# Layer B of a two-layer streaming encoder: the probabilities of head pairs 1 to 7 turned by DMA transposes in place of TensorE transposes

## The chip, the core and the metric

One Trainium2 chip, one core. The metric is the device time of one execution in microseconds (us). Three runs of the kernel before gave 2242.28, 2232.93 and 2240.86 us, a median of 2240.86 us. One further execution was recorded by the hardware profiler; all rows below are of that one.

## What is computed

Two attention layers over 2048 prompt tokens and 64 sample tokens, model width 1024. The change is in the second layer (layer B): 16 heads of 64 dimensions, a band of the token's own chunk and 8 earlier chunks of 64, a learned bias by clipped distance, and a gate. Cut to what matters:

```python
p = h @ w_in                                  # q, k, v, gate of layer B, 4 x 1024 columns
s = jnp.einsum('bqkgd,bskd->bkgqs', qg, k) * (dh ** -0.5) + bias
p = jax.nn.softmax(s, axis=-1)                # band of 9 chunks
o = jnp.einsum('bkgqs,bskd->bqkgd', p.astype(v.dtype), v)
y_p = x_p + (op * jax.nn.silu(gp)) @ w_out
```

All is float32 in the reference. The kernel gets there on TensorE by splitting a float32 operand into a high and a low part (here two float16 numbers) and multiplying both.

## The kernel before

**Stages.** Layer A's attention runs to about 0.69 ms of the profile, its output projection to about 0.9 ms, layer B's attention from there to about 2.08 ms, and the rest of layer B's output projection ends the program. Projections are not a stage of their own: `Filler` is a generator that hands out projection matmuls (`project`, L678 to L680, of 512 columns) a few at a time, and the pipelines of the two layers call `filler.to(mark)` between their own steps. The order of TensorE's instructions is therefore written out by hand (`manual_schedule` for PE); the other engines and the DMA queue of SyncE (SP), which issues every transfer, are ordered by a scheduler when the program is built.

**Layer B's pipeline.** `layer_b` makes one item for each head pair `hp` (0 to 7) and each unit of 256 tokens (8 units, each of two tiles of 128 tokens, and one sample item of 64 tokens). An item of a full unit has four steps, (tile i, head h) = (0,0), (1,0), (0,1), (1,1). A tile's band is up to five blocks of 128 keys: units 0 and 1 have 1, 2, 3 and 4 blocks for their tiles, all later ones 5. In one step:

- `scores` (L1408, L1409): four matmuls into a two-bank PSUM tile `sb`; VectorE adds the bias and takes the row minimum (L1412) into `p`, a 128x640 float32 tile of which there are three; ScalarE takes the exponential (L1416) and the row sum.
- one step later `values`: TensorE transposes each 128x128 float32 block of `p` into another `sb` tile (L840, the helper `transpose`); ScalarE writes the high part `ph` scaled by `PB` as float16 (L815), VectorE the low part `pl` (L816), both in `split_to`.
- after the second tile of a head, `products` (L1503): for each block of keys one matmul of `values` (held as `VH`) with `ph` and one with `pl`, 256 columns where both tiles see the block and 128 where one does. The first of them are put between the transposes of the next step's `values`; the rest, with two transposes of the gate `G` for the second head, follow them.
- at the end of the second head `finish_pairs` (L1243 to L1248) adds the halves, multiplies by the gate on GpSimd (POOL) and stores to `ogb`.

`queries` (L1347 to L1363) prepares the next item's q and k; `flush` issues copies of q (L1352) and stores held back. `Background` runs evacuation and normalisation work (`head_norm`: POOL at L755, L759 and L760, VectorE at L756 and L773) at fixed places; `anchor` names the ScalarE and VectorE instructions behind which such work is placed. Activations of layer B are loaded to `xx` from DRAM (L526, two transfers of 512 KB for each unit), through seven buffers. `VH` fills half of the `values` tile; the other half lies unused in layer B.

Of the kernel before, what the change touches and what calls it, by code (L numbers as in the profile page):

```python
# [11 lines left out]
F16 = mybir.dt.float16  # L12
I32 = mybir.dt.int32
AF = mybir.ActivationFunctionType
ALU = mybir.AluOpType
# [33 lines left out]
QY = 1  # L49
NS = 4  # L50
HB, WB_, PB, VB = 2.0 ** 10, 2.0 ** 14, 2.0 ** 14, 16.0
LAG = 3
HALF = 5 * 2 * P

@with_exitstack
def hybrid_encoder_kernel(
# [162 lines left out]
    def input_across(h):  # L219
        across(h, h + 1)  # L220
        e, r, o = row[:, 16:17], row[:, 17:18], row[:, 20:23]
        powers(row[:, h : h + 1], e, r)
        times(o[:, 0:1], r, WB_)
        times(o[:, 1:2], e, 1 / (HB * WB_))
        times(o[:, 2:3], e, 0.5 / (VB * PB))

    def input_scales(h):
        everywhere(h, row[:, 20:23])
# [581 lines left out]
    def split_to(dst_hi, dst_lo, src, scale=None):  # L810
# [7 lines left out]
            )  # L818
        return a, b

    def load_cache(ktsrc, vsrc, C, both):
# [12 lines left out]
        nt = C // P  # L834
        for c in range(nt):
            split_to(VS[:, c, :, 0:HD], VS[:, c, :, HD:P], rvv[:, c])
# [415 lines left out]
    def layer_b():  # L1252
# [4 lines left out]
        def add_unit(hp, unit):  # L1257
            u, T, tiles = unit
            it = Item()
            it.hp, it.unit, it.ready = hp, unit, False  # L1260
            its.append(it)
            last = u == NU
            cols = slice(2 * hp * HD, (2 * hp + 2) * HD)

            def prefetch():
                for j in range(NO):
                    assert finished["x1", j] == 2 or j * OT >= u * UT + T
                rows = None if hp else token_rows(unit)
                st.x[hp, u] = x = load_act(
                    x1, u * UT, T, False, T == TS, None, xs[1], hp > 0, F16, rows  # L1270
                )
                return x

            def weights(*m):
                if hp not in st.emit:
                    (st.w[hp],), _, st.emit[hp] = load_weights(1, (w_in_b[hp], 512), scale=gsb[:, hp])
                st.emit[hp](*m)

            def gen():
                xc = st.x.pop((hp, u))  # L1280
                it.prs, it.todo = [], []
                it.gate = t("pb", [P, 2, P], 5)
                if "VH" not in held:
                    held["VH"] = t("values", [P, NT, 2, P], 1, F16)
                for e, (tt, t0, n) in enumerate(tiles):
                    out = []
                    c = yield from project((tt, t0, n), xc, st.w[hp], 512, out)
                    if last:
                        pr, sums = evacuate_sample(hp, out[0], it.gate[:, e])
                        it.prs.append(pr)  # L1290
                        v, kn = pr[:n, 256:384], pr[n:, 0:128]
                        it.todo += [sums] + head_norm(P, pr[:, 0:128]) + gate(P, it.gate[:, e, 0:HD])
# [82 lines left out]
        def scores(it, i, h):  # L1375
# [35 lines left out]
            for r, b, c in soft:  # L1411
                mi = nc.vector.tensor_tensor_reduce(  # L1412
                    out=p[r, :nk], in0=S[r, o : o + nk], in1=b,
                    op0=ALU.add, op1=ALU.min, scale=1.0, scalar=3e38, accum_out=it.nm[r, c : c + 1],
                )
            ex = nc.scalar.activation(  # L1416
                p[:n, :nk], p[:n, :nk], AF.Exp,
                scale=-1.0, bias=it.nm[:n, c : c + 1], accum_out=it.sm[:n, c : c + 1],
            )
            bg.anchor(mi, ex)  # L1420
            if c == w - 1:
                nc.vector.reciprocal(it.sm[:n, :w], it.sm[:n, :w])
                it.G = G = t("G", [P, 256])
                if u == NU:
                    nc.gpsimd.tensor_tensor(
# [3 lines left out]
                for e in range(len(tiles)):  # L1429
                    nc.gpsimd.tensor_tensor(  # L1430
                        G[:n, e * P : (e + 1) * P].rearrange("p (h d) -> p h d", d=HD),
                        it.gate[:n, e].rearrange("p (h d) -> p h d", d=HD),
                        it.sm[:n, 2 * e : 2 * e + 2].unsqueeze(2).to_broadcast([n, 2, HD]),
                        op=ALU.mult,
                    )

        def values(it, i, h, short):
            u, T, tiles = it.unit
# [21 lines left out]
            ))  # L1460

        def then(it, i, h):
            if it.unit[0] == NU:
                return [([], lambda: sample_outputs(it)), ([], lambda: sample_turned(it))]
            if i == len(it.unit[2]) - 1:
                return [products(it, h)]
            return []

        def sample_outputs(it):
            O = psum("o", 512, 1)  # L1470
# [11 lines left out]
        def sample_turned(it):  # L1482
# [5 lines left out]
            store(og[1][:, it.hp, SEQ:TOK], o)  # L1488
            finished[1, NU] = finished.get((1, NU), 0) + 1

        def products(it, h):
            u, T, tiles = it.unit
            ta, tb = tiles[0][0], tiles[1][0]
# [16 lines left out]

            def rest():
                if h == 1:
                    n = tiles[0][2]
                    GT = psum("tp", 512, 1)
                    for e, (_, t0, _) in enumerate(tiles):
                        transpose(GT[:, t0 : t0 + n], it.G[:n, e * P : (e + 1) * P])
                    gt = gate_t(GT[:, :T].rearrange("p (j s) -> p j s", j=1), T, G_B(it.hp))
                for y, x in enumerate(full):
                    if y:
                        product(x, 0)  # L1520
                    product(x, 1, stop=y == last)
                if h == 1:
                    finish_pairs(
                        it.O[:, : 2 * T].rearrange("p (j e s) -> p j e s", j=1, e=2),
                        gt,
                        T,
                        og[1][:, it.hp : it.hp + 1, u * UT : u * UT + T],
                        True,
                    )
                    finished[1, u] = finished.get((1, u), 0) + 1  # L1530

            between = [begin]
            for x in short:
# [8 lines left out]
        def pipeline():  # L1542
# [7 lines left out]
            flush()  # L1550
            filler.to(its[1].mark)
            filler.attending = True
            prev, todo = None, []
            for x, it in enumerate(its):
                sample = it.unit[0] == NU
                heads = [(0, 0)] if sample else [(i, h) for h in range(2) for i in range(2)]
# [33 lines left out]
            values(*prev, [])  # L1590
            todo += then(*prev)
            while todo:
                filler.to(filler.done + 2.6)
                short, nxt = todo.pop(0)
                for fn in short:
                    fn()
                nxt()
            flush()

        return pipeline  # L1600
# [226 lines left out]
```

## Time and profile before

| | |
|---|---|
| median of three runs | 2240.86 us |
| profiled execution: its own time / span of its instructions | 2242.53 us / 2240.8 us |
| mean granted TensorE clock | 0.989 |
| share of the span busy: VectorE, ScalarE | 70%, 63% |
| share of time of the 16 DMA engines, SP's queue | 49.1% |
| bytes moved | 340.77 MB |

How to read it: TensorE's matmuls overlap one another, so the mean duration of a matmul in a group is longer than the time by which it moves the next one; the distance between the starts of neighbours in the timeline tells that. "Idle before" of a group is the idle time of its engine just before its instructions, with the instruction that ended it. SP's own row is a queue: a transfer that waits for a buffer holds up those behind it.

### The profile page before, as it was taken

The page shows a single profiled execution, that of the slowest core. Times are in us where ns is not written, and L with a number is a line of the kernel's source. Part 1 is how long each engine was busy: PE and PEld are TensorE (multiplying, and loading weights), DVE is VectorE, ACT ScalarE, POOL GpSimd, SP SyncE. Part 2 cuts the span into 40 slices and gives each one's busy share as a digit, 9 for nine tenths or more (in the row PEclk, how much of TensorE's full clock was granted, in tenths as well). Part 3 has the DMA queues.
Part 4 walks back from the last instruction along what each step waited for, and adds up shares of the span by engine and source line. Part 5 has one row for each costly group of instructions (what it writes and reads, how often), then busy time and mean ns, then how long its engine had stood idle before and what let it go on. Part 6 is the DMA issues. An engine that isn't in the chain of part 4 may idle for free.

```text
span 2240.8 us, 41683 instructions
## 1 busy us (share of the span) xinstructions
PE 2162.1 (96%) x13931; PEld 1580.2 (71%) x13931; DVE 1567.7 (70%) x4049; ACT 1419.6 (63%) x3610; POOL 858.4 (38%) x1397
## 2 busy tenths in 40 slices
PE   7999999999999999989999999999999999998999
PEld 6877888788889996556666666666566665566888
DVE  6768777667676456878776776867767777677542
ACT  6878778667785333666676666766666667566430
POOL 5545544334354456753333333332332323331000
PEclk9999999999999999999999999999999999999999
DMA  8856547756546666554243342533433424223664
GB/s 269 272 159 215 177 124 220 227 158 187 173 131 190 208 206 232 179 166 128 87 147 110 106 144 76 157 95 97 138 104 113 133 77 126 73 66 99 190 200 126
DMA packets 254072, 340.77 MB, mean 152 GB/s; under 512 B 45648, under 2 KB 191328, under 8 KB 253824
## 3 DMA queue, kind: packets, MB, share of 16 engines
q1 hardware_dynamic: 253856, 338.10, 49.1%
q8 instruction: 110, 1.80, 0.3%
q14 instruction: 106, 0.87, 0.1%
HBM read 257.59 MB, written 73.43 MB: 148 GB/s over the span
## 4 chain that ended last, share of the span: by engine, by line
PE 64%; DVE 13%; ACT 9%; DMA 6%; issue 5%; POOL 3%; SPq 1%; ACTq 0%; DVEq 0%; POOLq 0%
PE pj L678 11%; PE pj L680 11%; PE pj L679 11%; PE pj L1670 4%; PE pj L1672 4%; PE pj L1671 4%; PE sb L840 3%; PE o L1503 3%; PE tp L840 2%; DVE p L1412 2%; DMA scan<-in_w_in_b_dram 2%; PE sa L840 2%; ACT p L1416 2%; DVE pl L816 2%; PE sb L1408 1%
## 5 line engine op out<-in xcount | busy, mean ns | idle before, releaser
L678 PE MATMUL pj<-wh,xx 128*128 128x512 f16 (+2 forms) x1648 | 643.8, 391 | 6.2 <-ACT pb L701 4.8
L680 PE MATMUL pj<-wh,xx 128*128 128x512 f16 (+2 forms) x1648 | 626.1, 380 | 2.5 <-POOL xx L563 2.5
L679 PE MATMUL pj<-wh,xx 128*128 128x512 f16 x1024 | 390.5, 381 | 0.0
L1416 ACT ACTIVATE p<-p,nm 128x640 f32<-128x640 f32 (+5 forms) x264 | 199.5, 756 | 240.1 <-DVE nm L1412 237.5
L1670 PE MATMUL pj<-xx,wh 128*128 128x264 f32 (+1 forms) x1024 | 289.9, 283 | 5.2 <-DVE res L1676 2.2
L1671 PE MATMUL pj<-xx,wh 128*128 128x264 f32 (+1 forms) x1024 | 287.6, 281 | 0.0
L816 DVE SCALAR_TENSOR_TENSOR pl<-sb,ph 128x640 f16<-128x640 f32 (+4 forms) x256 | 189.0, 739 | 97.7 <-ACT ph L815 94.6
L679 PE MATMUL pj<-wl,xx 128*128 128x512 f32 (+1 forms) x624 | 235.7, 378 | 2.5 <-DVE wl L469 2.5
L563 POOL TENSOR_TENSOR xx<-xraw,xx 128x528 fp32r<-128x528 f32 (+4 forms) x144 | 183.9, 1296 | 87.8 <-ACT xx L562 72.8
L840 PE MATMUL sb<-ident,p 128*128 128x128 f32 x1144 | 207.6, 278 | 9.0 <-DVE pl L816 5.7
L1246 POOL TENSOR_TENSOR o<-gt,o 128x256 f32<-128x256 f32 (+1 forms) x132 | 99.9, 757 | 284.1 <-ACT p L1152 91.8
L1412 DVE CUSTOM_DVE_ANT_0 p<-sb,BT 128x640 f32<-128x640 f32 (+5 forms) x272 | 196.1, 721 | 15.5 <-PE sb L1409 10.4
L755 POOL TENSOR_TENSOR sq<-pa 128x256 f32<-128x256 f32 (+2 forms) x187 | 113.1, 605 | 226.0 <-ACT pa L714 152.5
L840 PEld LDWEIGHTS sb<-ident,p 128*128 128x128 f32 x1144 | 149.7, 142 | 68.5 <-DVE pl L816 20.7
L760 POOL TENSOR_TENSOR f<-f,mhalf 128x4 f32<-128x4 f32 (+2 forms) x187 | 192.3, 1028 | 14.1
L815 ACT ACTIVATE ph<-sb 128x640 f16<-128x640 f32 (+4 forms) x256 | 160.3, 626 | 49.8 <-PE sb L840 48.6
L680 PEld LDWEIGHTS <-xx 128*128 128x128 f16 x1024 | 100.7, 98 | 125.3 <-POOL xx L563 3.0
L1152 ACT ACTIVATE p<-p,nm 128x257 f32<-128x257 f32 (+2 forms) x272 | 134.3, 497 | 51.6 <-DVE nm L1146 44.3
L678 PEld LDWEIGHTS <-xx 128*128 128x128 f16 x1024 | 101.0, 99 | 71.4 <-issue 2.5
L679 PEld LDWEIGHTS <-xx 128*128 128x128 f16 x1024 | 100.7, 98 | 70.5 <-issue 2.3
L1503 PE MATMUL o<-pl,values 128*128 128x256 f16 (+1 forms) x672 | 149.5, 255 | 0.0
L1503 PEld LDWEIGHTS <-values 128*128 128x128 f16 x1344 | 134.8, 101 | 15.8 <-issue 0.2
(264 smaller groups left out, 5196.6 us busy)
## 6 DMA issues: line engine op xcount, KB each, us to landing
xx<-xsb SPq DMA_DIRECT2D x112, 512.0 KB, 3.8
xx<-xsa SPq DMA_DIRECT2D x88, 512.0 KB, 4.9
xraw<-oga SPq DMA_DIRECT2D x64, 264.0 KB, 3.8
xraw<-ogb SPq DMA_DIRECT2D x64, 264.0 KB, 3.8
xsa<-xx SPq DMA_DIRECT2D x32, 512.0 KB, 4.1
scan<-in_w_in_b_dram SPq DMA_DIRECT2D x64, 256.0 KB, 4.4
wl<-in_w_in_b_dram SPq DMA_DIRECT2D x64, 256.0 KB, 4.0
xraw<-in_x_dram SPq DMA_DIRECT2D x40, 256.0 KB, 3.9
```

Of the source, the lines that this page charges most:

```text
L563: nc.gpsimd.tensor_tensor(lo, rv, wide(hi), op=ALU.subtract)
L678: nc.tensor.matmul(ps[:n, :C], xh, wh, start=k == 0, stop=False)
L679: nc.tensor.matmul(ps[:n, :C], xh, wl, start=False, stop=False)
L680: nc.tensor.matmul(ps[:n, :C], xl, wh, start=False, stop=k == KC - 1)
L760: nc.gpsimd.tensor_tensor(fv, fv, mhalf[:n, :H], op=ALU.pow)
L816: b = nc.vector.scalar_tensor_tensor(dst_lo, src, scale, wide(dst_hi), op0=ALU.mult, op1=ALU.subtract)
L840: nc.tensor.transpose(out, in_, ident[:n, :n])
L1412: mi = nc.vector.tensor_tensor_reduce(out=p[r, :nk], in0=S[r, o : o + nk], in1=b, op0=ALU.add, op1=ALU.min, scale=1.0, scalar=3e38, accum_ ...
L1416: ex = nc.scalar.activation(p[:n, :nk], p[:n, :nk], AF.Exp, scale=-1.0, bias=it.nm[:n, c : c + 1], accum_out=it.sm[:n, c : c + 1],)
L1503: nc.tensor.matmul(it.O[:, h * T + q0 : h * T + q1_], vt, p[:, c, q0:q1_], start=start, stop=stop)
L1670: nc.tensor.matmul(ps[:, :OT], wh, oh, start=k == 0, stop=False)
L1671: nc.tensor.matmul(ps[:, :OT], wh, ol, start=False, stop=False)
```

## The change

For the full units of head pairs 1 to 7 (`turned`), both heads:

- right after the exponential, `parts` splits `p` without turning it: ScalarE copies it to float16, POOL subtracts that from `p` for the low part. Both go, block by block side by side, into one of three rotating slots in the unused half of `values`. The scale `PB` is put in before, by a small VectorE addition of log(PB) to the row's exponent.
- one step later `turn_p` issues one DMA transpose on SP for the tile: 128 x (2 x blocks x 128) float16 from the slot to a new tile `pt` (two buffers, one for each head).
- `turned_products` multiplies from `pt`, four steps (`LAG`) after the scores of a head's second tile. It has the same matmuls as before: a block seen by both tiles is read as two pieces of 128 columns.
- the gate's transposes take an `sb` tile in place of the `tp` tile; what is due when is kept in a list by step (`due`) in place of the pair `prev`, `todo`. For the sample items, and the gate scale, times and factors are adapted.

Head pair 0 and the sample items keep the TensorE transposes.

```diff
-LAG = 3
+LAG = 4
 HALF = 5 * 2 * P
+TURNED = (0, 1)
...
-                    held["VH"] = t("values", [P, NT, 2, P], 1, F16)
+                    held["VH"], held["two"] = (
+                        x.rearrange("p (a b c) -> p a b c", b=2, c=P)
+                        for x in split_at(t("values", [P, 4 * NT * P], 1, F16), 2 * NT * P)
+                    )
+                    held["turn"] = 0
...
+            if turned(it, h):
+                nc.vector.tensor_scalar(
+                    it.nm[:, c : c + 1], it.nm[:, c : c + 1], math.log(PB), 1.0,
+                    op0=ALU.add, op1=ALU.mult,
+                )
             ex = nc.scalar.activation(
...
             bg.anchor(mi, ex)
+            if turned(it, h):
+                parts(it, i, h, p, nk // P)
...
+        def turned(it, h):
+            return it.unit[0] != NU and it.hp > 0 and h in TURNED
+
+        def parts(it, i, h, p, m):
+            held["turn"] = r = (held["turn"] + 1) % 3
+            it.two = it.two if i else {}
+            it.two[i] = two = held["two"][:, 5 * r : 5 * r + m]
+            pv = p.rearrange("p (c q) -> p c q", q=P)[:, :m]
+            hi = nc.scalar.copy(two[:, :, 0, :], pv)
+            lo = nc.gpsimd.tensor_tensor(two[:, :, 1, :], pv, two[:, :, 0, :], op=ALU.subtract)
+            bg.anchor(hi, lo)
+            it.two[i] = two.rearrange("p c l q -> p (c l q)")
+
+        def turn_p(it, i, h, two):
+            if i == 0:
+                it.ph[h] = t("pt", [P, 2 * HALF], 2, F16)
+            m = two.shape[1]
+            nc.sync.dma_start_transpose(
+                it.ph[h][:, HALF * i : HALF * i + m].rearrange("p (c q) -> p c q", q=P), two
+            )
...
+            last = i == len(it.unit[2]) - 1
+            if turned(it, h):
+                two = it.two[i]
+                todo = [(1, "call", lambda: turn_p(it, i, h, two))]
+                return todo + [(LAG, "call", lambda: turned_products(it, h))] * last
+            return [(1, "values", (it, i, h))] + [(2 + late, "products", (it, h))] * last
...
+        def turned_products(it, h):
...
+            for kt in [kb] + [k for k in range(ka, tb + 1) if k != kb]:
+                for low in range(2):
+                    x, q0, q1_ = moving(kt, low)
+                    nc.tensor.matmul(
+                        it.O[:, h * T + q0 : h * T + q1_], held["VH"][:, kt, h], x,
+                        start=kt == kb and not low, stop=kt == tb and low == 1,
+                    )
+            if h == 1:
+                gates(it)
+                finish(it)
+
+        def gates(it):
+            u, T, tiles = it.unit
+            n = tiles[0][2]
+            GT = psum_b("sb", 1024, 2) if it.hp and len(TURNED) else psum("tp", 512, 1)
...
+            def due(at):
+                flush()
+                now = [x for x in todo if x[0] <= at]
+                todo[:] = [x for x in todo if x[0] > at]
...
                     scores(it, i, h)
                     bg.share(BL, BP_, KC)
                     goal(2 * y + 1)
-                    flush()
-                    short, nxt = todo.pop(0) if todo else ([], None)
-                    if prev is not None:
-                        values(*prev, short)
-                        bg.share(BL, BP_, KC)
-                        todo += then(*prev)
-                    prev = it, i, h
-                    if nxt is not None:
-                        nxt()
+                    due(step)
+                    todo += [(step + d, kind, o) for d, kind, o in then(it, i, h)]
+                    step += 1
```

More of the change, by code (lines that the diff above doesn't have):

```diff
@@ L224, in input_across @@
         times(o[:, 1:2], e, 1 / (HB * WB_))
-        times(o[:, 2:3], e, 0.5 / (VB * PB))
+        times(o[:, 2:3], e, 0.5 / VB if h > 0 and len(TURNED) == 2 else 0.5 / (VB * PB))
     def input_scales(h):
@@ L819, in split_to, with split_at @@
         return a, b
+    def split_at(x, c):
+        return x[:, :c], x[:, c:]
     def load_cache(ktsrc, vsrc, C, both):
@@ L1420, in scores @@
             bg.anchor(mi, ex)
+            if turned(it, h):
+                parts(it, i, h, p, nk // P)
             if c == w - 1:
                 nc.vector.reciprocal(it.sm[:n, :w], it.sm[:n, :w])
+                if turned(it, 0) and len(TURNED) == 1:
+                    part = it.sm[:n, TURNED[0] : w : 2]
+                    nc.vector.tensor_scalar(part, part, PB, 1.0, op0=ALU.mult, op1=ALU.mult)
                 it.G = G = t("G", [P, 256])
@@ L1462, in then @@
         def then(it, i, h):
+            late = it.hp > 0 and len(TURNED)
             if it.unit[0] == NU:
[L1464 to L1467, printed above, removed]
+                return [
+                    (1, "values", (it, i, h)), (2 + late, "call", lambda: sample_outputs(it)),
+                    (3 + late, "call", lambda: sample_turned(it)),
+                ]
+            last = i == len(it.unit[2]) - 1
[4 more added lines that the diff above has]
+            return [(1, "values", (it, i, h))] + [(2 + late, "products", (it, h))] * last
         def sample_outputs(it):
@@ L1489, in sample_turned, with moving, finish @@
             finished[1, NU] = finished.get((1, NU), 0) + 1
+        def turned_products(it, h):
+            u, T, tiles = it.unit
+            ta, tb = tiles[0][0], tiles[1][0]
+            ka, kb = max(ta - 4, 0), max(tb - 4, 0)
+            if h == 0:
+                it.O = psum("o", 512, 1)
+            def moving(kt, low):
+                if kt > ta:
+                    return it.ph[h][:, HALF + 2 * P * (kt - kb) + P * low :][:, :P], P, UT
+                c = it.ph[h][:, 2 * P * (kt - ka) + P * low :][:, :P]
+                if kt < kb:
+                    return c, 0, P
+                return (
+                    bass.AP(
+                        tensor=c.tensor, offset=c.offset,
+                        ap=[c.ap[0], [HALF - 2 * P * (kb - ka), 2], c.ap[-1]],
+                    ),
+                    0, UT,
+                )
[5 more added lines that the diff above has]
+                        start=kt == kb and not low, stop=kt == tb and low == 1,
+                    )
+            if h == 1:
+                gates(it)
+                finish(it)
+        def gates(it):
+            u, T, tiles = it.unit
+            n = tiles[0][2]
+            GT = psum_b("sb", 1024, 2) if it.hp and len(TURNED) else psum("tp", 512, 1)
+            for e, (_, t0, _) in enumerate(tiles):
+                transpose(GT[:, t0 : t0 + n], it.G[:n, e * P : (e + 1) * P])
+            it.gt = gate_t(GT[:, :T].rearrange("p (j s) -> p j s", j=1), T, G_B(it.hp))
+        def finish(it):
+            u, T, tiles = it.unit
+            finish_pairs(
+                it.O[:, : 2 * T].rearrange("p (j e s) -> p j e s", j=1, e=2),
+                it.gt,
+                T,
+                og[1][:, it.hp : it.hp + 1, u * UT : u * UT + T],
+                True,
+            )
+            finished[1, u] = finished.get((1, u), 0) + 1
         def products(it, h):
@@ L1512, in rest @@
                 if h == 1:
[L1513 to L1517, printed above, removed]
+                    gates(it)
                 for y, x in enumerate(full):
@@ L1522, in rest @@
                 if h == 1:
[L1523 to L1530, printed above, removed]
+                    finish(it)
             between = [begin]
@@ L1552, in pipeline @@
             filler.attending = True
-            prev, todo = None, []
+            todo, step = [], 0
+            def due(at):
+                flush()
+                now = [x for x in todo if x[0] <= at]
+                todo[:] = [x for x in todo if x[0] > at]
+                short, rests, vals = [], [], []
+                for _, kind, x in now:
+                    if kind == "products":
+                        between, rest = products(*x)
+                        short += between
+                        rests.append(rest)
+                    else:
+                        {"values": vals, "call": rests}[kind].append(x)
+                for x in vals:
+                    values(*x, short)
+                    bg.share(BL, BP_, KC)
+                for fn in short + rests:
+                    fn()
             for x, it in enumerate(its):
@@ L1589, in pipeline @@
                 assert x + 2 >= len(its) or its[x + 2].ready
-            values(*prev, [])
-            todo += then(*prev)
             while todo:
                 filler.to(filler.done + 2.6)
[L1594 to L1597, printed above, removed]
+                due(step)
+                step += 1
             flush()
```

## The prediction

> **What bounds the kernel now.** I read the page's first two parts first: who is busy, and whether the stage of the change differs from the mean.
>
> ```profile
> PE 2162.1 (96%) x13931; PEld 1580.2 (71%) x13931; DVE 1567.7 (70%) x4049; ACT 1419.6 (63%) x3610; POOL 858.4 (38%) x1397
> PE   7999999999999999989999999999999999998999
> POOL 5545544334354456753333333332332323331000
> DMA  8856547756546666554243342533433424223664
> ```
>
> TensorE (PE) is busy almost everywhere, in layer B's attention (slices 17 to 37) too. Then busy time by stretches: the steady part of layer B, and two stretches in which other engines are more loaded. The columns are busy us and instructions of PE, PEld, DVE, ACT and POOL, then granted clock, DMA share, GB/s.
>
> ```profile
> 200.00:300.00 100.00, 98.08 (x534) 78.72 (x533) 77.95 (x232) 82.51 (x224) 51.73 (x92) 0.98 0.57 181
> 900.00:1000.00 100.00, 91.18 (x549) 54.45 (x547) 79.22 (x181) 66.66 (x166) 66.14 (x83) 0.98 0.49 156
> 1000.00:2000.00 1000.00, 979.86 (x6155) 606.02 (x6156) 736.90 (x1850) 651.81 (x1665) 329.76 (x596) 0.99 0.37 112
> ```
>
> In the steady part PE idles 2.0%. So the PE work there sets the time, and work taken from PE shortens the stage until another resource is as long. Next the groups of that stretch with shapes kept apart, to get the length of one full unit and the cost of what moves:
>
> ```profile
> L1430 POOL TENSOR_TENSOR G<-pb,sm 128x128 f32<-128x128 f32 x110 | 46.1, 440 | 120.2 <-DVE sm L1422 84.2 <-PE sb L1409 21.7 <-PE tp L196 9.4
> L1425 POOL TENSOR_TENSOR G<-pb,sm 128x64 f32<-128x64 f32 x7 | 2.0, 292 | 38.9 <-DVE sm L1422 38.9
> L760 POOL TENSOR_TENSOR f<-f,mhalf 128x4 f32<-128x4 f32 x111 | 117.1, 1055 | 8.6
> L755 POOL TENSOR_TENSOR sq<-pa 128x256 f32<-128x256 f32 x111 | 68.0, 612 | 137.6 <-ACT pa L714 136.8
> L563 POOL TENSOR_TENSOR xx<-xraw,xx 128x512 f16<-128x512 f32 x3 | 3.6, 1212 | 0.0
> L1416 ACT ACTIVATE p<-p,nm 128x640 f32<-128x640 f32 x164 | 135.9, 829 | 140.7 <-DVE nm L1412 138.8 <-POOL sq L755 0.6
> L815 ACT ACTIVATE ph<-sb 128x640 f16<-128x640 f32 x163 | 113.0, 694 | 29.4 <-PE sb L840 28.8
> L466 ACT ACTIVATE wh<-wl,gsb 128x512 f16<-128x512 f32 x52 | 36.7, 715 | 0.0
> L816 DVE SCALAR_TENSOR_TENSOR pl<-sb,ph 128x640 f16<-128x640 f32 x163 | 134.0, 822 | 60.9 <-ACT ph L815 58.5
> L212 DVE COPY scl<-tp 128x3 f32<-128x3 f32 x7 | 1.1, 160 | 6.5 <-PE tp L211 6.3
> ```
>
> Two gate products (L1430) for each full unit: 55 units in 1000 us, with 7 sample items (L1425). A sample item I put at 4.6 us, an estimate from its 16 projection matmuls of 0.215 us (below) and about ten short ones. So a full unit takes (1000 - 7 x 4.6) / 55 = **17.6 us**, a step 4.4 us. By the shares of the stretch a unit holds 13.0 us of DVE, 11.5 of ACT, 5.8 of POOL and 6.4 of the 16 DMA engines (0.364 by the row further down).
>
> **The change part by part.** *Removed from PE.* Of the transposes of `p`,
>
> ```profile
> L840 PE MATMUL sb<-ident,p 128*128 128x128 f32 x1144 | 207.6, 278 | 9.0 <-DVE pl L816 5.7 <-DVE nm L1412 2.4
> ```
>
> 7 pairs x 2 heads x 70 blocks (1+2, 3+4, then six units of 5+5) = 980 go; 140 of pair 0 and 24 of the sample items stay. Their 278 ns overlap, so I take distances between starts in the timeline: five in a row up to the next projection, one between two products, and two short products next to each other.
>
> ```profile
> 1408.73 0.71 PE L840 MATMUL sb<-ident,p 128*128 128x128 f32 x5
> 1409.28 0.38 PE L678 MATMUL pj<-wh,xx 128*128 128x512 f16 x1
> 1409.49 0.38 PE L679 MATMUL pj<-wh,xx 128*128 128x512 f16 x1
> ...
> 2069.26 0.28 PE L840 MATMUL sb<-ident,p 128*128 128x128 f32 x1
> 2069.37 0.22 PE L1503 MATMUL o<-ph,values 128*128 128x128 f16 x1
> 2069.43 0.22 PE L1503 MATMUL o<-pl,values 128*128 128x128 f16 x1
> ```
>
> Five take 0.55 us, one 0.11 us either way. So 980 x 0.11 = **108 us**, 2.2 us for a unit of 20 blocks, 49 such units in all. The products keep their number and columns, and a short one costs 0.06 us without a transpose beside it too, so losing the interleaving costs PE nothing (the other end: 0.05 us each for 392, 20 us). The gate's transposes only change their tile. Head-pair projections, scores and the pacing marks stay as they are in PE's order.
>
> *DVE* loses L816, 4 x 0.82, and gains four additions of one column, by L212 0.16 each: 13.0 - 3.3 + 0.6 = 10.3 us a unit. *ACT* swaps a read of PSUM for one of SBUF: 0.69 us against 715 x 640/512 = 0.89, so 11.5 to 12.3. *POOL* gains four subtractions of 128x640; the same form at 512 columns took 1212 ns, so 1.5 us each: 5.8 + 6.1 = 11.9 us. PE itself comes to 17.6 x 0.98 - 2.2 = 15.05 us of work. So no engine is above PE, but POOL goes from a third to three quarters, in order, with waits between its parts. `parts` names its POOL instruction as an anchor too, so normalisation of later items (L755 to L760) now queues behind it; their results are due over a unit later, which hides it.
>
> *Added: 224 DMA transposes*, one a step, up to 128x1280 float16 = 320 KB (in binary KB). No row shows one. Nearest are plain transfers of that stretch (KB, us to landing) and their use of the engines:
>
> ```profile
> DMA packets 68074, 111.96 MB, mean 112 GB/s; under 512 B 10221, under 2 KB 39149, under 8 KB 67980
> q1 hardware_dynamic: 67980, 110.79, 36.4%
> xx<-xsb SPq DMA_DIRECT2D x108, 512.0 KB, 3.8
> scan<-in_w_in_b_dram SPq DMA_DIRECT2D x47, 256.0 KB, 4.4
> wl<-in_w_in_b_dram SPq DMA_DIRECT2D x40, 256.0 KB, 2.9
> q<-q SPq DMA_DIRECT2D x110, 32.0 KB, 2.2
> ```
>
> Low end: 327,680 bytes at 111 MB / 364 us = 304 GB/s make 1.1 us of engine time for a turn; 4 x 1.1 + 6.4 = 10.8 us a unit, hidden. High end: ten blocks one after the other as the 32 KB copy within SBUF, 22 us. Between them, as long as a plain transfer of its size takes to land: 2.9 to 3.8, so 3.1 us. The change gains nothing when four turns and the plain traffic fill the old unit: (17.6 - 6.4) / 4 = 2.8 us of exclusive time. I take 1.1 to 2.2 us, near the bytes, since the source rows are long, and keep the rest for a rival.
>
> The Trainium skill, DMA: Bandwidth & Descriptors, "Latency and other measured facts", gives DMA transposes an effective 261 GB/s in one kernel; as an estimate 1.3 us a turn, inside what I take. No run here shows it.
>
> *Added waits.* SP issues in order. A turn waits for POOL's low part, and for the first tile of a head also for the products of two heads before (two `pt` buffers). Behind it wait loads, weights, stores and the q copies; ahead of it stand loads that wait for a buffer:
>
> ```profile
> SPq L526 <- PE pj L680: 372.4, 73, 15.3
> ```
>
> 5.1 us in the mean, 15.3 at most. From the exponential a turn needs split 0.7, subtraction 1.5, landing 3 to 4: about 6 us and the queues, against four steps of 3.85 to the products. Three slots are shorter: the split of step s + 3 waits on ACT for the landing of step s, three steps = 11.5 us after its start. Slack 5 us. What idles PE instead I take from the stretches: 2% where POOL held 33% and ACT 65%, 2% with ACT at 83% and POOL at 52%, 9% at the stage's start with POOL at 66%. I take 5%: 15.05 / 0.95 = 15.84 us a unit, a gain of 1.76 x 49 = 86 us. With 2% it is 110, with 9% it is 52. At the end, two more steps of lag are filled by output projection matmuls at hand: nothing.
>
> **Sum.** 2242.5 (the profiled execution: span 2240.8 and 1.7 around it) - 86 = 2156.5; it lies 1.7 above the median of the three runs, so **2155 us**. Its own range is 2125 (2% idle, rounded out) to 2228 (nearly all the gain lost in waits).
>
> **Rivals.** *1, slower: the turns hold the DMA engines and become the bound.* For it: every row with 32 KB or more lands in 2 us or later, and the turned data is written in pieces that no plain transfer here has. Against: plain engine time is 1.1 us for these bytes. It decides from 2.8 us a turn. At 3.1 us a unit is 4 x 3.1 + 6.4 = 18.8 us: +1.2 x 49 = +59, **2300 us**; at 3.6 us it is 2400. At the high end of 22 us it would be near 6000 (94.4 us a unit); of this rival's 0.30, 0.04 lie at that end.
>
> The Trainium skill, VectorE: DVE Perf Modes, "The three transpose paths", speaks against the change: a 128x128 bf16 turn by DMA takes 1309 ns, by TensorE 390. Ten in series would be an estimate of 13.1 us a turn, 58.8 us a unit, some 4260 us; the trace's 0.11 us for a TensorE transpose in a row shows that such single figures need not add up in series.
>
> *2, slower: waits in order, not work.* The slot is freed late, ACT stops at a split, evacuations behind it stop, and PE waits for a PSUM tile. The chain is split 0.7, POOL behind L760 and L755 1.7, subtraction 1.5, SP queue x, landing 3.8; over three steps it passes 4.4 us at x = 5.5, close to the mean 5.1 of SP's waits. At x = 7 a step is 14.7 / 3 = 4.9, a unit 19.6: +2.0 x 49 = +98, **2340 us**. Against it: 73 waits in 55 units are fewer than the 220 turns, and the built order puts the turns among the loads.
>
> *3, same:* x near 5.5, or a turn near 2.8 us: about **2241 us**.
>
> *4, it doesn't do what it says:* no: the built instruction lists have 980 fewer transposes of `p`, 224 DMA transposes, and 1176 products from `pt`.
>
> **How the numbers follow.** Forecast 0.45, rival 1 0.30, rival 2 0.18, rival 3 0.07. The likeliest gives 2155. For 8 in 10 the range runs from 2125 through both slower rivals to 2400, leaving out some 0.13 above (long turns) and 0.05 below. Beyond 0.5% either way (11 us, about what a measurement of this kernel can tell from no change): faster 0.45, same 0.07, slower 0.48.
>
> **What would show it.** Right: PE near 95% from 1000 us on, a unit near 15.8 us, turns landing in 3 to 5 us, DMA share near 0.7. Rival 1: DMA slices at 9, PE waiting in `turned_products` for a transfer. Rival 2: ACT idle before the new copy, with DMA as releaser, and SP waiting before its turns. The sum is wrong, too, if POOL's subtraction takes far more than 1.5 us, or if loads of `xx` come late behind the turns.

## The result, and the profile after

The changed kernel took 2265.32 us in the median of four runs (2263.27 to 2268.36), the kernel before 2238.56 us beside it: a ratio of 1.0123, 95% interval 1.0095 to 1.015. It is slower by 1.2%, where 3.8% less was forecast. The profiled execution took 2266.93 us over a span of 2265.1 us.

The page after: TensorE's row, and the granted clock in 40 slices.

```profile
PE 2091.1 (92%) x12951; PEld 1478.5 (65%) x12951; DVE 1535.1 (68%) x4049; ACT 1434.4 (63%) x3610; POOL 1142.3 (50%) x1621
...
PEclk9999999999999999999999999999999998998999
```

The 980 transposes are gone from the count (13931 to 12951), and yet the span grew. Span and busy time account for it: PE was idle for 2240.8 - 2162.1 = 78.7 us before and for 2265.1 - 2091.1 = 174.0 us after, **95 us more**. Its busy time fell by 71 us, not 108: **37 us** of what was left took longer. 95 + 37 - 108 = +24, the difference of the two spans. The mean granted clock fell from 0.989 to 0.971, which by itself makes 2091 us of work some 38 us longer. The steady stretch shows both (busy us by engine, clock, DMA share, GB/s):

```profile
1000.00:2000.00 1000.00, 892.57 (x5115) 499.99 (x5113) 690.25 (x1810) 645.23 (x1621) 567.38 (x779) 0.96 0.70 166
```

PE idles 10.7% there, not 2.0, and the granted clock is 0.96 in place of 0.99. No engine is full. For whom PE waits in that stretch (us in total, times, longest), first after, then before:

```profile
PE tp L844 <- DVE pa L774: 34.2, 14, 5.3
PE pj L679 <- ACT wh L467: 21.8, 13, 4.3
PE pj L680 <- DVE wh L470: 17.6, 18, 1.5
PE sb L1416 <- DVE nm L1420: 8.1, 5, 2.2
```

```profile
PE tp L840 <- DVE scl L212: 4.7, 5, 1.1
PE sb L840 <- DVE pl L816: 4.7, 16, 0.9
```

Of the 107 us that PE idles there after, 34.2 + 21.8 + 17.6 = 73.6 us are waits for two things that the diff does not seem to touch: `pa`, the normalised q and k of the next item, and `wh`, the split weights of the next head pair. No wait for a transpose stands there.

How a wait costs twice is read from windows of 5 us around the longest one:

```profile
1435.00:1440.00 5.00, 5.00 (x33) 2.97 (x32) 2.56 (x2) 3.13 (x6) 4.44 (x4) 1.00 1.12 251
1440.00:1445.00 5.00, 0.49 (x4) 0.18 (x2) 3.61 (x11) 0.41 (x1) 1.02 (x2) 1.00 0.79 203
1445.00:1450.00 5.00, 4.22 (x15) 2.09 (x16) 3.12 (x9) 4.24 (x11) 3.62 (x7) 0.66 0.93 240
1450.00:1455.00 5.00, 5.00 (x35) 3.08 (x34) 2.19 (x8) 3.65 (x8) 2.41 (x4) 1.00 0.87 168
```

PE stands still for 5.3 us; in the 5 us behind that the granted clock is 0.66, and 15 matmuls pass where 33 did before (the first 0.8 us of this window are still idle; after that, projection matmuls start 0.43 us apart, not 0.22). The Trainium skill, TensorE: Matmul & The Clock Gate, "Part 1: The HAM clock gate", says that an idle window of about 3.4 us halves the clock until the array has been busy as long again; this trace agrees: from 1446 to 1449 us the granted clock is 0.50, and 0.66 is the mean of half speed for 3.4 of 5 us.

What VectorE (DVE) did in that gap, from the timeline:

```profile
1441.10 0.69 DVE L175 TENSOR_REDUCE most<-scan 128x1 f32<-128x512 f32 x1 [2.92 <-DMA scan<-in_w_in_b_dram]
1441.71 0.81 DVE L1420 CUSTOM_DVE_ANT_0 p<-sb,BT 128x640 f32<-128x640 f32 x1
...
1443.42 0.40 DVE L757 TENSOR_REDUCE f<-sq 128x4 f32<-128x256 f32 x1
...
1445.31 0.41 DVE L774 TENSOR_TENSOR pa<-pa,f 128x256 f32<-128x256 f32 x1
```

The normalisation (L757, POOL's power, L774) was put in the queue so late that anything ahead of it, here a reduction waiting for its load, went straight into PE's wait.

The groups of the stretch that answer to the priced operations, after; then, of before, the three on VectorE that both kernels have:

```profile
L1464 POOL TENSOR_TENSOR values<-p,values 128x640 f16<-128x640 f32 x147 | 208.0, 1415 | 137.1 <-ACT values L1463 134.6 <-DMA q<-q 1.9
L1463 ACT CAST values<-p 128x640 f16<-128x640 f32 x147 | 106.1, 722 | 3.0
L783 DVE SCALAR_TENSOR_TENSOR pb<-sq,pb 128x128 f32<-128x128 f32 x107 | 73.7, 689 | 38.8 <-ACT sq L782 38.4
L470 DVE SCALAR_TENSOR_TENSOR wh<-wl,gsb,wh 128x512 f16<-128x512 f32 x52 | 64.8, 1246 | 27.5 <-ACT wh L467 27.5
L774 DVE TENSOR_TENSOR pa<-pa,f 128x256 f32<-128x256 f32 x107 | 63.7, 595 | 36.0 <-POOL f L761 34.5
```

```profile
L773 DVE TENSOR_TENSOR pa<-pa,f 128x256 f32<-128x256 f32 x111 | 49.3, 444 | 25.5 <-POOL f L760 24.9
L469 DVE SCALAR_TENSOR_TENSOR wh<-wl,gsb,wh 128x512 f16<-128x512 f32 x52 | 38.8, 756 | 5.6 <-ACT wh L466 5.6
L782 DVE SCALAR_TENSOR_TENSOR pb<-sq,pb 128x128 f32<-128x128 f32 x110 | 31.6, 291 | 3.6 <-ACT sq L781 2.7
```

The split and the subtraction took what was estimated (0.72 and 1.42 us). But three VectorE operations of unchanged shape, whose two tensors both lie in SBUF, got longer: 291 to 689 ns, 756 to 1246, 444 to 595. The transfers of the stretch:

```profile
q1 hardware_dynamic: 295547, 164.74, 69.7%
xx<-xsb SPq DMA_DIRECT2D x106, 512.0 KB, 4.2
wl<-in_w_in_b_dram SPq DMA_DIRECT2D x40, 256.0 KB, 3.7
q<-q SPq DMA_DIRECT2D x108, 32.0 KB, 2.5
pt<-values SPq DMA_TRANSPOSE x202, 3.8
```

A turn lands in 3.8 us (the median of all sizes). The engines' share rose from 36.4% to 69.7%; with 0.354 for the plain traffic (by 107 normalisations in place of 110) that is 343 us over 202 turns, 1.7 us each. As an estimate, by the mean of 4.3 blocks, a full turn of five takes 2.0.

### The profile page after: what moved, and what is told of

Its sections match the earlier page's. It is cut to its first block, busy times and chain, and to the rows that moved or that the text cites. A ratio compares the mean times of both kernels' runs of the same rounds, so it can differ in the third digit from the quotient of the medians.

```text
span 2265.1 us, 40934 instructions
## 1 busy us (share of the span) xinstructions
PE 2091.1 (92%) x12951; PEld 1478.5 (65%) x12951; DVE 1535.1 (68%) x4049; ACT 1434.4 (63%) x3610; POOL 1142.3 (50%) x1621
## 4 chain that ended last, share of the span: by engine, by line
PE 50%; DVE 17%; ACT 11%; DMA 8%; issue 7%; POOL 6%; SPq 1%; ACTq 0%; POOLq 0%; DVEq 0%
PE pj L680 8%; PE pj L681 8%; PE pj L679 8%; PE pj L1765 4%; PE pj L1767 4%; PE pj L1766 4%; DMA scan<-in_w_in_b_dram 3%; DVE p L1420 3%; ACT p L1429 2%; PE sa L844 2%; ACT values L1463 2%; DVE wh L470 2%; DVE pb L783 2%; PE tp L844 2%; POOL values L1464 2%
## 5 line engine op out<-in xcount | busy, mean ns | idle before, releaser
L679 PE MATMUL pj<-wh,xx 128*128 128x512 f16 (+2 forms) x1648 | 651.9, 396 | 26.3 <-ACT wh L467 21.8
L681 PE MATMUL pj<-wh,xx 128*128 128x512 f16 (+2 forms) x1648 | 634.9, 385 | 2.5 <-POOL xx L564 2.5
L680 PE MATMUL pj<-wh,xx 128*128 128x512 f16 x1024 | 401.0, 392 | 17.6 <-DVE wh L470 17.6
L1464 POOL TENSOR_TENSOR values<-p,values 128x640 f16<-128x640 f32 (+2 forms) x224 | 282.3, 1261 | 224.1 <-ACT values L1463 221.4
L1420 DVE CUSTOM_DVE_ANT_0 p<-sb,BT 128x640 f32<-128x640 f32 (+5 forms) x272 | 195.4, 718 | 61.8 <-PE sb L1417 58.8
L681 PEld LDWEIGHTS <-xx 128*128 128x128 f16 x1024 | 102.7, 100 | 152.0 <-issue 35.8
L680 PEld LDWEIGHTS <-xx 128*128 128x128 f16 x1024 | 102.6, 100 | 109.1 <-issue 37.2
L774 DVE TENSOR_TENSOR pa<-pa,f 128x256 f32<-128x256 f32 (+3 forms) x221 | 127.9, 579 | 54.1 <-POOL f L761 49.0
L679 PEld LDWEIGHTS <-xx 128*128 128x128 f16 x1024 | 103.0, 101 | 86.6 <-issue 12.1
L783 DVE SCALAR_TENSOR_TENSOR pb<-sq,pb 128x128 f32<-128x128 f32 (+3 forms) x204 | 121.9, 597 | 55.5 <-ACT sq L782 54.3
L756 POOL TENSOR_TENSOR sq<-pa 128x256 f32<-128x256 f32 (+2 forms) x187 | 125.1, 671 | 55.2 <-ACT pa L702 26.9
L1463 ACT CAST values<-p 128x640 f16<-128x640 f32 (+2 forms) x224 | 146.9, 656 | 4.9
L1767 PE MATMUL pj<-xx,wl 128*128 128x264 f32 x512 | 145.8, 285 | 0.9 <-DVE wl L463 0.9
L1767 PE MATMUL pj<-xx,wh 128*128 128x264 f16 x512 | 143.0, 279 | 1.0 <-DVE wh L460 1.0
```

Source lines behind the costliest of these rows:

```text
L679: nc.tensor.matmul(ps[:n, :C], xh, wh, start=k == 0, stop=False)
L680: nc.tensor.matmul(ps[:n, :C], xh, wl, start=False, stop=False)
L681: nc.tensor.matmul(ps[:n, :C], xl, wh, start=False, stop=k == KC - 1)
L1420: mi = nc.vector.tensor_tensor_reduce(out=p[r, :nk], in0=S[r, o : o + nk], in1=b, op0=ALU.add, op1=ALU.min, scale=1.0, scalar=3e38, accum_ ...
L1463: hi = nc.scalar.copy(two[:, :, 0, :], pv)
L1464: lo = nc.gpsimd.tensor_tensor(two[:, :, 1, :], pv, two[:, :, 0, :], op=ALU.subtract)
```

## The experiments

All were compared with the kernel before on the same chip; ratios have 95% intervals.

**Theory A** came from reading the diff again for what it takes out. Before, a step calls `bg.share`, which hands out background work (weight splits, normalisation), once behind `scores` and once behind `values`. In the new `due` the second call stands in the loop over `vals`, and turned heads have none. A step hands out half as much. The built order shows it: on ScalarE the last four of the eight weight splits for head pair 5 (counted from 0) stand behind softmaxes 155, 155, 155 and 156 of layer B before, and behind 156, 157, 158 and 159 after. **Theory B** was that the turns' DMA time and POOL's load make the waits, **theory C** that POOL's subtraction slows VectorE.

### The dropped call put back

```diff
                 for x in vals:
                     values(*x, short)
                     bg.share(BL, BP_, KC)
+                if now and not vals:
+                    bg.share(BL, BP_, KC)
```

> The changed kernel with one more call of bg.share in each step in which only turned heads are due, so that background work is handed out twice a step again, as before the change. Theory A (the change dropped that call, so weight splits and normalisation are emitted late and PE waits for them, 39 us for wh and 36 us for pa, and runs at a lower granted clock after each wait): most of those waits go, PE is over 94% busy from 1100 to 2000 us, the clock there is back at 0.98, the time falls by 50 to 90 us to 2175 to 2215, faster than before. Theory B (the transposes' DMA time and POOL's load make the waits): the waits stay, 2250 to 2270. Theory C (VectorE slowed by POOL's subtraction is what is late): a small gain, 2245 to 2260.

2220.91 us, 0.9921 (0.9904 to 0.9937): 44 us less than the changed kernel, and now faster than before. The four weight splits stand behind softmaxes 155, 155, 155 and 156 again. The steady stretch and PE's waits in it:

```profile
1000.00:2000.00 1000.00, 912.27 (x5311) 518.07 (x5309) 722.08 (x1865) 670.81 (x1681) 586.93 (x806) 0.97 0.71 171
```

```profile
PE tp L844 <- DVE pa L774: 18.4, 9, 3.8
PE sb L1416 <- DMA q<-q: 16.1, 8, 3.7
PE tp L844 <- DVE scl L213: 12.3, 5, 2.5
PE o L844 <- POOL o L1526: 12.3, 6, 2.9
```

The waits for `wh` are gone and those for `pa` half. But PE still idles 8.8%, and new waits are at the top. The gain lies just under A's range of 50 to 90 us: A is right and not the whole.

### The call left out of the kernel before

```diff
                         values(*prev, short)
-                        bg.share(BL, BP_, KC)
+                        if prev[0].hp == 0 or prev[0].unit[0] == NU:
+                            bg.share(BL, BP_, KC)
```

> The kernel before, with the second call of bg.share of a step left out for the full units of head pairs 1 to 7: the dropped call alone, with no DMA transpose and no subtraction on POOL. Theory A: slower than before by 30 to 90 us (2270 to 2330), with PE waits for wh and pa at the borders of head pairs. Theories B and C: within 10 us of before.

2251.39 us, 1.0075 (1.0049 to 1.0101). The weight splits stand as in the changed kernel (behind 156, 157, 158 and 159), and with no transposes by DMA the same wait for `wh` appears, smaller:

```profile
PE pj L678 <- ACT wh L466: 11.3, 6, 2.0
PE sb L840 <- DVE nm L1412: 6.4, 7, 1.6
```

14 us here against 44 there: less than A expected (30 to 90) and more than B and C did (within 10). No wait for `pa` stands in the stretch, so the dropped call alone does not make normalisation late; it takes what the change adds as well. That late work costs more where the engines that do it are slower and PE is faster would explain the rest, and was not tested apart.

### A plain copy in place of the turn

```diff
-            nc.sync.dma_start_transpose(
-                it.ph[h][:, HALF * i : HALF * i + m].rearrange("p (c q) -> p c q", q=P), two
-            )
+            nc.sync.dma_start(it.ph[h][:, HALF * i : HALF * i + m], two)
```

> The changed kernel with each DMA transpose replaced by a plain DMA of the same bytes from the same slot to the same buffer: the turn itself is left out, so the products are of unturned blocks. Theory B: the engines' share falls well under 0.72 from 1100 to 2000 us and the time falls by 20 us or more (2245 or less). Theories A and C: the time stays within 8 us of 2265, with the same waits for wh and pa.

2260.99 us, 1.0109 (1.0084 to 1.0134): 4 us less than with the turn, with the same waits (31.7 us for `pa`, 17.1 and 15.7 for `wh`). The same edit on the better version below, at 2201.0 us:

> The version at 2201 us with each DMA transpose replaced by a plain DMA of the same bytes; the turn is left out, so the products are of unturned blocks. If the turns' engine time (2.0 us each by the shares, against 1.1 for a plain copy) still costs something once the background work is handed out in time: 10 to 25 us less, 2176 to 2191. If not: within 6 us of 2201, as it was 4 us on the changed kernel.

2199.27 us, 0.9835 (0.9813 to 0.9857), with the engines' share at 0.52 in the steady stretch in place of 0.73:

```profile
1000.00:2000.00 1000.00, 922.09 (x5419) 524.08 (x5420) 733.70 (x1910) 744.31 (x1840) 604.42 (x828) 0.98 0.52 172
```

Theory B's first half falls as far as the turning goes: it costs some 0.2 of the engines' time, and 4 and 2 us of the kernel's, no more than the noise. What the transfers cost even as plain copies was not tested; no run leaves them out.

### The subtraction on VectorE

```diff
-            lo = nc.gpsimd.tensor_tensor(two[:, :, 1, :], pv, two[:, :, 0, :], op=ALU.subtract)
+            lo = nc.vector.tensor_tensor(two[:, :, 1, :], pv, two[:, :, 0, :], op=ALU.subtract)
```

> The changed kernel with the low part subtracted on VectorE in place of POOL. Theory C: VectorE's operations with two operands in SBUF go back to their lengths before (wh L470 from 1.29 to 0.76 us, pb L783 from 0.71 to 0.29, pa L774 from 0.61 to 0.44), and the time falls by 15 us or more (2250 or less). Theory A: the waits for wh and pa stay about as they are, the time is within 10 us of 2265. If VectorE with four more operations of 0.7 us a unit becomes late itself, the time rises.

2283.89 us, 1.0208 (1.019 to 1.0226), 19 us more than the changed kernel, though VectorE's other operations went back to their lengths:

```profile
L1464 DVE TENSOR_TENSOR values<-p,values 128x640 f16<-128x640 f32 x144 | 124.5, 864 | 78.4 <-ACT values L1463 77.1
L470 DVE SCALAR_TENSOR_TENSOR wh<-wl,gsb,wh 128x512 f16<-128x512 f32 x52 | 39.6, 761 | 0.2
L783 DVE SCALAR_TENSOR_TENSOR pb<-sq,pb 128x128 f32<-128x128 f32 x104 | 29.3, 286 | 1.5 <-ACT sq L782 0.9
```

This shows the cause of the lengthening: it is there with the subtraction on POOL and gone without it. The Trainium skill, GPSIMD Engine Reference, "1. Specifications", says that POOL shares its SBUF interfaces with VectorE, with contention where VectorE has two SBUF inputs; these rows agree. PE's wait for `pa` is gone too, but those for `wh` stay (41.5 us), and waits for `KB` and `pb`, both from VectorE, come to 48. So the stretched operations did not make the waits for the weights. What the stretching costs by itself this run cannot say, because it gives VectorE the subtractions as well.

### What still holds PE once the call is back

Three theories for the rest: D, the order on POOL (the subtraction is named as an anchor, and normalisation has to queue behind it); E, the q copies in SP's queue; F, that POOL and VectorE simply hold more. Each edit is on top of the restored call (2220.91 us).

```diff
-            bg.anchor(hi, lo)
+            bg.anchor(hi)
```

> The changed kernel with the call of bg.share restored (2220.9 us, the base here) and POOL's subtraction no longer named as an anchor, so that normalisation need not be placed behind it. Theory D (what still keeps PE waiting is the order on POOL: pa, scl and the sample's o are late behind subtractions): the waits for pa fall from 21 us to under 8, the time by 8 to 25 us, 2196 to 2213. Theory E (SP's queue: the q copies behind the transposes) and theory F (VectorE and POOL simply hold more work for a unit): within 6 us of 2221.

2224.15 us, 0.9929 (0.9902 to 0.9955): no gain. The wait for `pa` is no longer among the largest; the row minimum of the softmax took its place:

```profile
PE sb L1416 <- DVE nm L1420: 26.1, 18, 2.2
PE sb L1416 <- DMA q<-q: 13.7, 5, 3.0
```

The copies of q made by ScalarE from PSUM, as the kernel did already for its last two items:

```diff
-            if it not in its[-2:]:
+            direct = it.hp > 0 or it in its[-2:]
+            if not direct:
                 held["later"].append(copies)
```

> The changed kernel with the call of bg.share restored and the copies of q for head pairs 1 to 7 made by ScalarE from PSUM (two operations of 0.47 us a unit) in place of two transfers on SP's queue. Theory E: the waits of the scores for q copies (16 us) go, the time falls by 8 to 20 us, 2201 to 2213. Theories D and F: within 6 us of 2221, or slower by ScalarE's 0.9 us a unit where it is the late one.

2215.3 us, 0.989 (0.9869 to 0.9911): 6 us, less than E's 8 to 20. The waits for these transfers are gone, but PE now waits for ScalarE's copies (`q`, L1377), 27.5 us in the scores and 16.5 for the `tp` tile, and still 17.7 for `pa`. Both edits together:

> The changed kernel with the call of bg.share restored, the subtraction no anchor and the q copies on ScalarE: theories D and E together. If both hold, 2185 to 2205; if neither, within 8 us of 2221.

2201.0 us, 0.984 (0.9821 to 0.986): 20 us less than with the call alone, where the two edits alone gave -3 and 6. PE 917 of 1000 us busy, clock 0.98:

```profile
1000.00:2000.00 1000.00, 917.47 (x5413) 521.78 (x5413) 734.90 (x1914) 747.57 (x1843) 603.38 (x828) 0.98 0.73 172
```

D and E hold only jointly. That with one late chain mended the other is next is our reading of the lists. The q copies on ScalarE's DMA queue, on top of the version without the anchor:

```diff
-                    load(wide(q1[hh][halves[1 - hh]]), wide(q1[hh][rows]))
+                    (nc.scalar.dma_start if it.hp else load)(wide(q1[hh][halves[1 - hh]]), wide(q1[hh][rows]))
```

> The changed kernel with the call of bg.share restored and no anchor on POOL (2224 us), with the copies of q of head pairs 1 to 7 issued on ScalarE's DMA queue in place of SyncE's: the same transfers, not behind the transposes in the issuing queue. Theory E' (it is the place in SP's queue that made the q copies late): PE's waits for q go, 2190 to 2210, at or below the version that copies on ScalarE. Theory E'' (it is the DMA engines, busy with the turns, that make them late): within 8 us of 2224.

2230.49 us, 0.998 (0.9966 to 0.9994): 6 us more than without this edit. PE's wait for the copies stayed (13.0 us, 13.7 from SP), and from 1100 to 2000 us they landed later than from SP (2.2 us there):

```profile
q<-q ACTq DMA_DIRECT2D x98, 32.0 KB, 3.7
```

So another queue than SP's does not cure them; why they are late stays open.

### Half of the turns

```diff
-TURNED = (0, 1)
+TURNED = (1,)
```

> The changed kernel with the call of bg.share restored and only the second head of each pair turned by DMA; the first head goes through TensorE transposes again: half the transposes' TensorE time is saved (54 us), POOL has two subtractions of 1.4 us less for a unit, the queue two transposes less. Theory F: PE over 95% busy, the time at or below 2221, 2190 to 2215. Theories D and E: the waits halve and so does the saving, 2215 to 2235.

2230.42 us, 0.9968 (0.9952 to 0.9984). (The factor `PB` on the turned head's row sums, one VectorE operation on two columns a unit, is left out in this kernel.) PE was 946 of 1000 us busy, but with half of its transposes kept. Half the change gave 8 us, the whole, with the same call, 16: the two points fit a gain that goes with the number of turns. The time lies in the range of D and E (2215 to 2235), not in that of F (2190 to 2215).

### POOL's part

On top of the version at 2201.0 us, POOL subtracts one block a tile (the low parts of the others are left out, and the slots are set to zero once):

```diff
-            lo = nc.gpsimd.tensor_tensor(two[:, :, 1, :], pv, two[:, :, 0, :], op=ALU.subtract)
+            lo = nc.gpsimd.tensor_tensor(two[:, 0:1, 1, :], pv[:, 0:1], two[:, 0:1, 0, :], op=ALU.subtract)
```

> The version at 2201 us (call of bg.share restored, no anchor on POOL, q copies on ScalarE) with POOL subtracting only one block of each tile in place of up to five; the low part of the other blocks is left out (zeros or older data). Everything else, the transposes' size too, stays. Theory F (POOL's load of 1.4 us a step, and what it does to VectorE's operations with two operands in SBUF, hold the rest of the saving): pb and wh on VectorE shrink towards 0.29 and 0.76 us, PE's idle time from 1100 to 2000 us falls from 81 to under 45 us, the time by 25 to 55 us, 2145 to 2175. Theory G (the rest is latency of chains that do not pass POOL): within 10 us of 2201.

2168.23 us, 0.9693 (0.967 to 0.9716): 33 us less. The steady stretch:

```profile
1000.00:2000.00 1000.00, 941.43 (x5636) 545.84 (x5636) 677.65 (x1966) 768.21 (x1890) 431.89 (x846) 0.98 0.76 178
```

VectorE's `pb`, `wh` and `pa` took 329, 771 and 490 ns there, near their lengths before the change. F holds for these 33 us on this base. Whether through POOL's own length or through VectorE's, two more kernels asked, with the subtraction on VectorE for a pair's first head, and for both heads:

```diff
-            lo = nc.gpsimd.tensor_tensor(two[:, :, 1, :], pv, two[:, :, 0, :], op=ALU.subtract)
+            lo = (nc.vector, nc.gpsimd)[h].tensor_tensor(two[:, :, 1, :], pv, two[:, :, 0, :], op=ALU.subtract)
```

> The version at 2201 us with the subtraction of a pair's first head on VectorE and of its second on POOL. If POOL's queue and the slowed VectorE are what costs, a balance helps: 2180 to 2197. If VectorE is at its limit already (73% busy, with the row minimum that every softmax waits for), its two more operations of 0.87 us a unit cost as much as POOL's save: 2195 to 2215.

For both heads the line is that of the kernel with the subtraction on VectorE above.

> The version at 2201 us with all subtractions on VectorE: no long POOL operation beside it, VectorE's pb and wh back at 0.29 and 0.76 us. If the slowing of VectorE by POOL is the cost: 2165 to 2190. If the cost is VectorE's order and load: slower than 2201, 2205 to 2240.

For the first head alone 2225.28 us, 0.9941 (0.9918 to 0.9964), 24 us more than at 2201.0 and outside both ranges; for both 2189.18 us, 0.9775 (0.974 to 0.9809), 12 less, and the fastest kernel of this study that does the whole computation:

```profile
1000.00:2000.00 1000.00, 928.93 (x5503) 530.46 (x5504) 789.32 (x2153) 753.25 (x1867) 378.42 (x623) 0.98 0.74 174
```

VectorE is 79% busy there and PE's idle time less. So in this version VectorE does better with a longer list at full speed than with a shorter one slowed by POOL. On the changed kernel the same edit lost 19 us; which of the three edits between the two turns the sign was not tested. Why the mixture loses is open.

### Three steps in place of four

```diff
-LAG = 4
+LAG = 3
```

> The version at 2201 us with the products three steps behind the scores in place of four. If the transposes land as early as their 3.8 us say (split, subtraction and queue about 7 us after the scores' end), PE does not wait for pt with three steps either: within 6 us of 2201. If the fourth step is needed (queues in front of the transposes), PE waits for pt and the time rises by 15 us or more.

On the version at 2201.0 us: 2269.46 us, 1.0145 (1.0125 to 1.0164), 68 us more. At the top of PE's waits stands the one for the turned tile, which came to 6.2 us at most in the four-step kernels whose waits are told of here:

```profile
PE o L1562 <- DMA pt<-values: 41.0, 17, 7.5
```

The fourth step is needed. The turn's 3.8 us alone do not fill three steps of about 4.3 us. That the queues ahead of it do is the likely rest, and was not measured apart.

## Why the prediction was wrong

- *The sum* took 108 us of work off PE and gave back 22 for more idle time (5%, not 2%). Measured, 95 of idle time and 37 of slower work came back. The range of 2125 to 2400 holds 2265 only because it ran through the slower rivals, and neither of these, as written, is what happened: that is luck.
- *The bound and the saving* were right. PE did bound the kernel, and 980 x 0.11 = 108 us were there: busy time fell by 2162.1 - 2059.8 = 102 us in the version with least waiting.
- *"A turn takes 1.1 to 2.2 us of engine time, lands in 3 to 4"*: 2.0 and 3.8. The estimate of 1.3 us was too low, that of 13.1 us, ten blocks in series, far too long. With the plain copy in its place the kernel was 4 us shorter, so rival 1 did not happen. (Not every row of 32 KB or more landed in 2 us or later, as it has it: before, 32 KB stores to `ogb` landed in 1.4.)
- *Split and subtraction*: 0.72 and 1.42 us against 0.7 to 0.9 and 1.5. Right.
- **The step that failed is the list of what the change removes.** It named transposes and VectorE's splits, not the second `bg.share` of a step, which hung on `values`. It stood in the diff. On it rested the sentence that normalisation's "results are due over a unit later, which hides it": the work is handed out late, and PE waited 34 us for it and 39 for weights. Putting the call back gained 44 us, took the waits for weights away and left 18 us for normalisation. That rest went when POOL's subtraction was no longer an anchor, so the queueing behind it, which the same sentence put at nothing, was not hidden either; by itself, though, that edit brought no time.
- **The price of the waits was mis-sized.** 5% idle was taken from stretches with busy engines; it was 10.7%, and still 8.8% with the call back. What made it so beside the dropped call, as far as shown: the q copies and POOL's anchor together, 20 us; the subtraction on POOL, 33 us. That an idle PE also runs slower afterwards, 37 us here, was not in the sum at all.
- *Rival 2* had the sign and the kind (waits in order), but its place was wrong: ScalarE had no wait for a transfer in the stretch, and the three slots were enough.
- *Not settled:* the version with least waiting is at 2168, some 38 us above 2238 - 108 = 2130 (its missing subtractions aside). Its larger waits are for the q copies now on ScalarE, 21.6 us in the scores and 18.3 for the PSUM tile `tp` that the copies read; no kernel undid that.

## What to carry to other kernels

When an operation leaves a hand-written order, list everything that hung on its place there, calls that hand out other work too, and ask when that work is done now. Work taken from the bounding engine shortens only what the other engines can follow; add up each chain in their queues against the new, shorter step, not their busy shares. And count a wait of the bounding engine with the slower clock after it.

## What the runs showed of the hardware that was not expected

- DMA transposes within SBUF, most of them of 128x1280 float16, landed in 3.8 us in the median beside other traffic; one of full size took about 2.0 us of the 16 engines. Plain copies of as many bytes, in the version at 2199.27 us, landed in 2.9 us.
- A long POOL subtraction with two SBUF operands stretched VectorE operations with two SBUF operands, 291 to 689 ns and 756 to 1246; one with an operand in PSUM stayed (L1412 before, L1420 after: 820 and 815 ns).
- After 5.3 us of idle TensorE the granted clock was 0.66 over the next 5 us; over the stretch it came to 0.96 against 0.99.
